# Pairing the weight-stationary steps of a Mamba-2 / attention trunk, and its decay differences on ScalarE

## The chip, the cores and the metric

The kernel runs on one core of one Trainium2 chip. The metric is the time of one execution on the device in microseconds (us); before the change the median of three runs is 2558.26 us (2557.04 to 2558.56).

## The reference

Two decoder layers over 256 tokens of width 2048, all in float32: a Mamba-2 mixer with a conv-gated feed-forward network, then block attention with another one. Nearly all the work is products of the 256 tokens with large weight matrices. The part that the change rewrites, besides the products, is the decay inside one chunk of 128 tokens:

```python
a_cum = jnp.cumsum(a, axis=2)
seg = a_cum[:, :, :, None] - a_cum[:, :, None, :]
decay_in = jnp.exp(jnp.where(causal, seg, -jnp.inf))
cb = jnp.einsum('bclgn,bcsgn->bclsg', c, b)
y_diag = jnp.einsum('bclsgr,bcsgrp->bclgrp', cb[..., None] * decay_in, x)
...
u = causal_dwconv(x @ w_up, conv_w, conv_b)
return (jax.nn.silu(gate) * val) @ w_down
```

There are 8 groups of 8 heads and two chunks of 128 tokens, so a group has 2 x 8 difference matrices of 128x128.

## The kernel before

**Products.** Weights come from HBM in tiles of 512 KB (`raw`, one per *step*; 882 steps). `split()` turns a tile into two: ScalarE casts it to `hi` (fp32r, L183), VectorE subtracts to get the rest `lo` (L184), and the next load is issued on SyncE's queue. Activations are kept the same way, as a hi half and a lo half side by side (`hT`). A product is hi·hi + lo·hi + hi·lo.

A *chunk* of steps computes 512 columns. In mode "X" the activations are the stationary operand and the weight tile streams, 12 matmuls of 512 columns a step (L206, L207, L211). In mode "W" the weights are stationary: for each of a step's eight 128x128 blocks there is one matmul of `hi` with both halves of the activations, 512 columns (L243), and one of `lo` with the hi half, 256 columns (L245). A "W" chunk has eight steps, the first four into one PSUM pair and the last four into another. `whole(i)` issues a step: in even steps the eight of `hi` and then the eight of `lo`, in odd steps the other way round, so that runs of sixteen of a kind arise. 61 chunks are of this sort: 3 for B and C and 8 for x in the Mamba layer, 42 in the two feed-forward networks, 8 for keys and queries. The first chunk (`both`) and the small one for dt (mode "H") are cut otherwise.

**Order of the work.** The program is one list of steps. In the middle of a step (after 6 of its 16 matmuls) `splits(i)` issues the split three steps ahead; there are four buffers each for `hi` and `lo`, and a split needs the buffers of the step four before it. Work of the layers is hung on steps by hand: `at(i, f)` runs f after step i. Every engine works its own list in the order of issue.

**Mamba.** Group g has an x chunk (steps `s0` to `s0+7`, mode "W") and a z chunk (`s0+8` to `s0+15`, mode "X"). Its work is hung at `s0+k`:

- `s0+3` `m_load`: DMAs on GpSimd's queue put the cumulative sums, the same for all partitions, into `mA`, one 128x1024 tile for each of two chunks of tokens (2 buffers).
- `s0+6` `m_cb`: three small matmuls (L673, L674), then `cb` on VectorE (L676) and `bc` on ScalarE (L680); `m_decay` for chunk 0: VectorE subtracts `aux` from `mA` (L685) and takes the minimum with 0 (L686). `s0+7`: the same for chunk 1, and `m_exp` for chunk 0 (ScalarE, L690); `s0+8` `m_exp` for chunk 1.
- `s0+4`, `s0+5` and `s0+8`, `s0+9`: `gather` (L550, L551) and `taps` of the convolution (ScalarE L573, then VectorE L578).
- `s0+12` silu; `s0+13`, `s0+14` the mask; `s0+15` to `s0+29` the rest of the group beside the next group's steps, among it `y_off` and `y_diag` (PE L732, L724) after the next group's third and fourth step, `z_gate` (VectorE L744, ScalarE L747) after its sixth, `z_rms` after its seventh and `z_turn` (PE L340) after the fifth and sixth steps of its z chunk.

The time steps of all groups (dt) are worked out beside the chunks of C; `dt_turn` (PE L647) comes after the third step of the second of them and needs an exponential on ScalarE (L640, L641).

Of the kernel before, what the change touches and what calls it, by code (L numbers as in the profile page):

```python
# [20 lines left out]
AF = mybir.ActivationFunctionType  # L21
OP = mybir.AluOpType
AX = mybir.AxisListType

P = 128
D = 2048
S = 256
# [31 lines left out]
def chunks():  # L59

    z, b, c, dt = 0, 2 * DI, 2 * DI + NG * DS, 2 * DI + 2 * NG * DS

    def some(mode, name, layer, c0, n, nk):
        return [(mode, name, layer, c0 + i * NC, nk, False) for i in range(n)]

    def ffn(layer):
        up = [some(m, "ffn_w_up", layer, c + j * NC, 1, KD)[0] for j in range(DFF // NC)
              for m, c in (("W" if j else "X", 0), ("W", DFF))]
        return up + some("X", "ffn_w_down", layer, 0, 4, KF)

    out = some("W", "mamba_w_in", 0, b, 2, KD)
    out[0] = out[0][:5] + (True,)
    out += some("H", "mamba_w_in", 0, dt, 1, KD) + some("W", "mamba_w_in", 0, c, 2, KD)
    for g in range(NG):
        out += some("W", "mamba_w_in", 0, DI + g * NC, 1, KD) + some("X", "mamba_w_in", 0, z + g * NC, 1, KD)
    out += some("X", "mamba_w_out", 0, 0, 4, DI // P) + ffn(0)
    out += some("X", "w_kv", None, D, 1, KD) + some("W", "w_kv", None, 0, 4, KD) + some("W", "attn_w_q", 0, 0, 4, KD)
    return out + some("X", "w_kv", None, D + NC, 3, KD) + some("X", "attn_w_o", 0, 0, 4, KD) + ffn(1)


def cut(mode, nk, both):

    if mode == "H":
        return [(0, NC // 8, k, 8) for k in range(0, nk, 8)]
    if mode == "W" and not both:
        return [(half, HC, k, 4) for half in (0, HC) for k in range(0, nk, 4)]
    return [(0, NC, k, 2) for k in range(0, nk, 2)]
# [3 lines left out]
def yoco_kernel(ctx: ExitStack, tc: tile.TileContext, x, lmg, lmb, lfg, lfb, x_t, columns, w, out):  # L91
    nc = tc.nc
# [10 lines left out]
    def acc_pair():  # L103
        return psum.tile([P, 2, NC], F32, tag="acc", name="acc", bufs=3)
# [19 lines left out]
    steps, plan = [], chunks()  # L124

    class Chunk:
# [9 lines left out]
        def __init__(self, x, head=0, tail=0):  # L136
            self.mode, _, _, _, self.nk, self.both = plan.pop(0)
            self.x, self.head, self.tail = x, head, tail
            self.cut = cut(self.mode, self.nk, self.both)
            self.n = len(self.cut)  # L140
            self.per = self.cut[0][3]
            self.nj = max(self.cut[0][1] // P, 1)
            self.first = len(steps)
            for s in range(self.n):
                steps.append((self, s))
            self.end = len(steps)
            self.last = self.end - 1

        def place(self, s):

            return self.cut[s][2], self.cut[s][0] // HC

        def ready(self, half):

            return self.end - (self.n // 2 if half == 0 and not self.both else 0)

    raw_t, hi_t, lo_t = {}, {}, {}
    spare = {}
    calm = []
# [12 lines left out]
    def split():  # L172
        i = pos["split"]
        pos["split"] += 1
        t = raw_t.pop(i)
        if i in spare:
            h, l = (bufs["h"][:, k:k + 2].rearrange("p k a t -> p k (a t)") for k in (spare[i], spare[i] + 2))
        else:
            h = wts.tile([P, 2, NC], F32R, tag="hi", name="hi")
            l = wts.tile([P, 2, NC], F32R, tag="lo", name="lo")  # L180
        for e in ((0,), (1,)) if i < 2 else ((0, 1),):
            sl = slice(e[0], e[-1] + 1)
            nc.scalar.copy(h[:, sl], t[:, sl])  # L183
            nc.vector.tensor_sub(l[:, sl], t[:, sl], h[:, sl].bitcast(F32))  # L184
        hi_t[i], lo_t[i] = h, l
        load()

    def splits(i, most=2):

        for _ in range(1 if steps[i][0] in calm else most):  # L190
            j = pos["split"]
            ahead = LA + 1 + sum(i <= k < j for k in spare)
            if j < min(i + ahead, n_steps) and (j in spare or sum(k not in spare for k in hi_t) < LA + 1):
                split()
# [27 lines left out]
    def done(i):  # L222
        hi_t.pop(i), lo_t.pop(i)

    def whole(i):
        ch, s = steps[i]
        h, l = hi_t[i], lo_t[i]
        nj = ch.nj
        h, l = (t.rearrange("p a (k n) -> p (a k) n", n=nj * P) for t in (h, l))
        k0, half = ch.place(s)  # L230
        banks = [p[:, j, :] for p in ch.part[half:] for j in range(2)]

        parts = (1, 0) if s % 2 and ch not in calm else (0, 1)
        order = [(p, kk, j) for p in parts for kk in range(ch.per) for j in range(nj)]
        for n, (p, kk, j) in enumerate(order):
            if n == len(order) * 3 // 8:
                run(mid, i)
                splits(i)
            k = k0 + kk
            begins, ends = k == 0 and p == parts[0], k == ch.nk - 1 and p == parts[1]  # L240
            js = slice(j * P, (j + 1) * P)
            if p == 0:
                nc.tensor.matmul(banks[j], h[:, kk, js], ch.x.both(k), start=begins, stop=ends, skip_group_check=True)  # L243
            else:
                nc.tensor.matmul(banks[j][:, :S], l[:, kk, js], ch.x.hi(k), start=begins, stop=ends,  # L245
                                 skip_group_check=True)

    def products(i):
        ch, s = steps[i]
        if ch.mode == "W":  # L250
            if s == 0:
                ch.part = []
            if s == 0 or (not ch.both and s == ch.n // 2):
                ch.part += [acc_pair() for _ in range(1 + ch.both)]
        elif s == 0:
            a = acc_pair()
            ch.part = [a[:, 0, :], a[:, 1, :]] if ch.mode == "X" else [a]
            if ch.tail:
                ch.part.pop()
                ch.piece = [tp_tile()[:, :HC] if ch.tail == LAST else acc_pair()[:, 0, :HC] for _ in range(2)]  # L260
        if ch.mode != "X":
            whole(i)
            return done(i)
        half(i, 0)
        if i >= ch.end - ch.tail:
            if i < ch.last:
                return splits(i)
            for q in range(2):
                for j in range(ch.end - ch.tail, ch.end):
                    half(j, 1, q)  # L270
                    if q:
                        done(j)
        elif s < ch.head - 1:
            if ch.tail:
                splits(i)
        elif s == ch.head - 1:
            for j in range(ch.first, i + 1):
                if j < i or ch.tail:
                    splits(i, 1)
                second(j)  # L280
                done(j)
            if not ch.tail:
                splits(i, 1)
        else:
            run(mid, i)
            splits(i)
            second(i)
            done(i)

    post, pre, mid, inner, outer = {}, {}, {}, {}, {}  # L290

    def run(d, i):
        for f, a in d.get(i, []):
            f(*a)

    def at(i, f, *a):
        post.setdefault(i, []).append((f, a))
# [246 lines left out]
    aux = mp.tile([P, 6, NH], F32, name="aux")  # L544
# [136 lines left out]
        G[g]["cb"], G[g]["bc"] = cb, bc  # L681

    def m_decay(g, c):
        t = G[g]["A", c]
        nc.vector.tensor_sub(t, t, aux[:, 2 + c, 8 * g:8 * g + 8].unsqueeze(2).to_broadcast([P, 8, P]))  # L685
        nc.vector.tensor_scalar(t, t, 0.0, None, op0=OP.min)  # L686

    def m_exp(g, c):
        t = G[g]["A", c]
        nc.scalar.activation(t, t, AF.Exp)  # L690

    def m_mask(g, c):
        t = G[g]["A", c]
# [81 lines left out]
    for g in range(NG):  # L775
        s0 = chX[g].first
        at(s0 + 3, m_load, g)
        at(s0 + 6, m_cb, g)
        at(s0 + 6, m_decay, g, 0)
        at(s0 + 7, m_decay, g, 1)  # L780
        at(s0 + 7, m_exp, g, 0)
        at(s0 + 8, m_exp, g, 1)
        conv4(chX[g], 4 * g, lambda g=g: x_new(g), 0).plan()
        at(s0 + 12, x_silu, g)
        at(s0 + 13, m_mask, g, 0)
        at(s0 + 14, m_mask, g, 1)
        at(s0 + 15, x_turn, g)
        at(s0 + 16, x_dt, g)
        at(s0 + 16, z_silu, g)
        at(s0 + 18, y_off, g)  # L790
        at(s0 + 18, y_diag, g, 0)
        at(s0 + 19, y_diag, g, 1)
        at(s0 + 21, z_gate, g)
        at(s0 + 22, z_rms, g)
        at(s0 + 23, z_scale, g)
        at(s0 + 28, z_turn, g, 0)
        at(s0 + 29, z_turn, g, 1)
# [213 lines left out]
    for h in range(HEADS):  # L1011
        i, j = divmod(h, 4)
# [87 lines left out]
```

## Time and profile before

| | |
|---|---|
| median of three runs | 2558.26 us |
| the profiled execution: its time / its span | 2558.33 us / 2556.4 us |
| granted TensorE clock | 0.999 |
| TensorE (PE) busy | 99% |
| VectorE (DVE) / ScalarE (ACT) busy | 65% / 51% |
| share of the DMA engines, mean rate | 61%, 196 GB/s |
| the chain that ended last | PE 98%, DVE 1% |

Busy shares are of the span. Matmuls overlap in the pipeline, so a PE that is busy all the time can still have lost time between matmuls; start-to-start times tell it. In rows of the timeline the columns are start, duration of the merged instructions, engine, line, operation, out<-in, shapes, count, and in brackets how long the engine sat idle before and what ended that.

### The profile page before, as it was taken

What the parts mean: (1) busy time and instruction counts of PE and PEld (TensorE: products, weight loads), DVE (VectorE), ACT (ScalarE), POOL (GpSimd) and SP (SyncE); (2) the same over time, 40 slices, a digit from 0 to 9 for tenths busy, and PEclk for the clock granted to TensorE, in tenths of its full rate; (3) what the DMA queues carried; (4) which work ended last, traced back from release to release, by engine and by line L of the source; (5) the groups of instructions that cost most, each with busy time, mean ns of one, the idle gap of its engine ahead of it and who ended that gap; (6) DMA issues with size and microseconds to landing.
All of it is one profiled execution on the core that took longest, in us unless ns stands there. A gap on an engine that the chain in (4) does not pass through costs nothing.

```text
span 2556.4 us, 35404 instructions
## 1 busy us (share of the span) xinstructions
PE 2543.6 (99%) x13744; PEld 2199.0 (86%) x13744; DVE 1666.5 (65%) x2138; ACT 1300.0 (51%) x1634; POOL 72.3 (3%) x87
## 2 busy tenths in 40 slices
PE   9999999999999999999999999999999999999998
PEld 8888888888888888888888888888888888888887
DVE  6877788854676666666444745655777676765545
ACT  6656556633465555555333444543555555554333
POOL 0000000000200000000000200000200000000001
PEclk9999999999999999999999999999999999999999
DMA  7555555557566565666676655456665666566675
GB/s 260 197 186 188 189 179 186 192 186 234 185 228 190 187 190 184 194 192 190 199 229 199 222 190 173 157 173 223 222 197 187 192 186 192 185 195 200 198 224 163
DMA packets 141495, 500.98 MB, mean 196 GB/s; under 512 B 15616, under 2 KB 16128, under 8 KB 141328
## 3 DMA queue, kind: packets, MB, share of 16 engines
q1 hardware_dynamic: 136976, 483.46, 58.8%
q0 software_dynamic: 4064, 14.75, 1.8%
q8 instruction: 107, 1.75, 0.3%
q14 instruction: 60, 0.49, 0.1%
q10 hardware_dynamic: 288, 0.52, 0.1%
HBM read 490.22 MB, written 8.45 MB: 195 GB/s over the span
## 4 chain that ended last, share of the span: by engine, by line
PE 98%; DVE 1%; issue 0%; ACT 0%; DMA 0%; SPq 0%; DVEq 0%
PE acc L243 36%; PE acc L245 19%; PE acc L211 13%; PE acc L206 13%; PE acc L207 13%; PE tp L724 1%; PE tp L211 0%; PE tp L207 0%; PE tp L206 0%; DVE lo L184 0%; PE tp L340 0%; PE tp L708 0%; PE tp L965 0%; PE tp L732 0%; DVE r L417 0%
## 5 line engine op out<-in xcount | busy, mean ns | idle before, releaser
L184 DVE TENSOR_TENSOR lo<-raw,hi 128x1024 fp32r<-128x1024 f32 (+1 forms) x871 | 1063.2, 1226 | 732.2 <-ACT hi L183 728.3
L183 ACT CAST hi<-raw 128x1024 fp32r<-128x1024 f32 (+1 forms) x871 | 912.6, 1049 | 915.6 <-PE acc L211 377.4
L243 PE MATMUL acc<-hT,hi 128*128 128x512 f32 x3984 | 961.4, 392 | 0.4 <-ACT hi L183 0.4
L243 PEld LDWEIGHTS acc<-hT,hi 128*128 128x128 f32 x3984 | 731.0, 188 | 141.7 <-ACT hi L183 1.0
L245 PEld LDWEIGHTS acc<-hT,lo 128*128 128x128 f32 x3984 | 512.5, 191 | 20.0
L245 PE MATMUL acc<-hT,lo 128*128 128x256 f32 x3984 | 522.5, 283 | 0.0
L207 PE MATMUL acc<-lo,gT 128*128 128x512 f32 (+1 forms) x678 | 254.5, 378 | 0.0
L206 PE MATMUL acc<-hi,gT 128*128 128x512 f32 (+1 forms) x678 | 254.1, 377 | 0.0
L211 PE MATMUL acc<-hi,gT 128*128 128x512 f32 (+1 forms) x678 | 200.8, 377 | 0.0
L206 PE MATMUL acc<-hi,hT 128*128 128x512 f32 x448 | 179.9, 402 | 0.0
L207 PE MATMUL acc<-lo,hT 128*128 128x512 f32 x448 | 175.2, 391 | 0.0
L207 PEld LDWEIGHTS acc<-lo,gT 128*128 128x128 f32 x678 | 127.7, 188 | 23.4
L206 PEld LDWEIGHTS acc<-hi,gT 128*128 128x128 f32 x678 | 127.5, 188 | 23.0
L211 PEld LDWEIGHTS acc<-hi,gT 128*128 128x128 f32 x678 | 124.9, 188 | 23.7
L211 PE MATMUL acc<-hi,hT 128*128 128x512 f32 x448 | 139.4, 392 | 0.6 <-DVE hT L353 0.6
L211 PEld LDWEIGHTS acc<-hi,hT 128*128 128x128 f32 x448 | 83.4, 188 | 20.5 <-DVE hT L353 3.0
L206 PEld LDWEIGHTS acc<-hi,hT 128*128 128x128 f32 x448 | 84.2, 188 | 17.2 <-ACT hT L352 1.3
L206 PE MATMUL acc<-hi,yT 128*128 128x512 f32 (+1 forms) x270 | 98.9, 371 | 0.0
L207 PEld LDWEIGHTS acc<-lo,hT 128*128 128x128 f32 x448 | 84.3, 188 | 16.9 <-DVE lo L184 0.9
L207 PE MATMUL acc<-lo,yT 128*128 128x512 f32 (+1 forms) x270 | 98.6, 369 | 0.0
L211 PE MATMUL acc<-hi,yT 128*128 128x512 f32 (+1 forms) x270 | 77.7, 369 | 0.0
L578 DVE SCALAR_TENSOR_TENSOR g<-u,cols,g 128x254 f32<-128x254 f32 (+1 forms) x176 | 73.5, 478 | 5.3 <-ACT g L573 5.3
(200 smaller groups left out, 1875.6 us busy)
## 6 DMA issues: line engine op xcount, KB each, us to landing
raw<-in_w SPq DMA_DIRECT2D x881, 512.0 KB, 4.1
mA<-acum_d POOLq DMA_DIRECT2D x16, 512.0 KB, 5.2
hres<-r POOLq DMA_DIRECT2D x12, 512.0 KB, 6.3
r<-hres SPq DMA_DIRECT2D x12, 512.0 KB, 5.1
r<-in_x SPq DMA_DIRECT2D x4, 512.0 KB, 5.2
gb<-in_ln_mix_g SPq DMA_DIRECT2D x8, 256.0 KB, 6.0
gb<-in_ln_mix_b SPq DMA_DIRECT2D x8, 256.0 KB, 6.4
gb<-in_ln_ffn_g SPq DMA_DIRECT2D x8, 256.0 KB, 5.5
```

Of the source, the lines that this page charges most:

```text
L183: nc.scalar.copy(h[:, sl], t[:, sl])
L184: nc.vector.tensor_sub(l[:, sl], t[:, sl], h[:, sl].bitcast(F32))
L206: nc.tensor.matmul(a, th, h[:, kk, sl], start=k == 0, stop=False)
L207: nc.tensor.matmul(a, th, l[:, kk, sl], start=False, stop=False)
L211: nc.tensor.matmul(a, ch.x.lo(k)[:, ts], h[:, kk, sl], start=False, stop=k == ch.nk - 1)
L243: nc.tensor.matmul(banks[j], h[:, kk, js], ch.x.both(k), start=begins, stop=ends, skip_group_check=True)
L245: nc.tensor.matmul(banks[j][:, :S], l[:, kk, js], ch.x.hi(k), start=begins, stop=ends, skip_group_check=True)
L578: nc.vector.scalar_tensor_tensor(d, u[:, i % 2, :S - k], c1(self.at_w, w[n - 1 - k] + self.ia + i), d, op0=OP.mult, op1=OP.add)
L724: nc.tensor.matmul(ps[:, h * 64:(h + 1) * 64], G[g]["A", c][:, h, :], G[g]["xdt"][:, c, h * 64:(h + 1) * 64], start=True, stop=True)
```

## The change

Two edits. **Pairs:** in the 61 chunks of mode "W" the steps are issued two by two. The even step of a pair issues the first kind of product for both steps (sixteen matmuls), the odd step the second kind for both. The first and third pair of a chunk begin with `hi`, the second and fourth with `lo`. The even step's tiles are given up in the middle of the odd step, and the odd step's split is issued there. **Decays:** `m_decay` becomes eight ScalarE activations, one for each head (128x128, Relu of `-mA + aux`, with a bias of one value per partition); `m_exp` takes the sign back with a scale of -1 and moves one step later, to `s0+8` and `s0+9`.

```diff
+            self.paired = self.mode == "W" and not self.both
...
+        def kinds(self, s):
+            return (1, 0) if (s // 2 if self.paired else s) % 2 and self not in calm else (0, 1)
...
-    def whole(i):
-        parts = (1, 0) if s % 2 and ch not in calm else (0, 1)
-        order = [(p, kk, j) for p in parts for kk in range(ch.per) for j in range(nj)]
-        for n, (p, kk, j) in enumerate(order):
-            if n == len(order) * 3 // 8:
-                run(mid, i)
-                splits(i)
...
+    def whole(i):
+        ch, s = steps[i]
+        a, b = ch.kinds(s)
+        if not ch.paired:
+            order = [(s, a), (s, b)]
+        elif s % 2 == 0:
+            order = [(s, a), (s + 1, a)]
+        else:
+            order = [(s - 1, b), (s, b)]
+        late = ch.paired and s % 2
+        n = len(order) * ch.per * ch.nj
+        c = 0
+        for t, p in order:
+            for _ in some(ch, t, p):
+                if c == (n // 2 if late else n * 3 // 8):
+                    if late:
+                        done(i - 1)
+                    run(mid, i)
+                    splits(i)
+                c += 1
+        if not ch.paired or late:
+            done(i)
...
     def m_decay(g, c):
         t = G[g]["A", c]
-        nc.vector.tensor_sub(t, t, aux[:, 2 + c, 8 * g:8 * g + 8].unsqueeze(2).to_broadcast([P, 8, P]))
-        nc.vector.tensor_scalar(t, t, 0.0, None, op0=OP.min)
+        for h in range(8):
+            nc.scalar.activation(t[:, h, :], t[:, h, :], AF.Relu, scale=-1.0, bias=aux[:, 2 + c, 8 * g + h:8 * g + h + 1])
...
-        nc.scalar.activation(t, t, AF.Exp)
+        nc.scalar.activation(t, t, AF.Exp, scale=-1.0)
...
-        at(s0 + 7, m_exp, g, 0)
-        at(s0 + 8, m_exp, g, 1)
+        at(s0 + 8, m_exp, g, 0)
+        at(s0 + 9, m_exp, g, 1)
```

`some(ch, s, p)` yields before each matmul of step s and kind p; the matmuls themselves are those of before.

More of the change, by code (lines that the diff above doesn't have):

```diff
@@ L223, in done, with some @@
         hi_t.pop(i), lo_t.pop(i)
+    def some(ch, s, p):
+        i = ch.first + s
+        nj = ch.nj
+        w = ((hi_t, lo_t)[p][i]).rearrange("p a (k n) -> p (a k) n", n=nj * P)
+        k0, half = ch.place(s)
+        banks = [p[:, j, :] for p in ch.part[half:] for j in range(2)]
+        first = ch.kinds(s)[0] == p
+        for kk in range(ch.per):
+            k = k0 + kk
+            begins, ends = first and k == 0, not first and k == ch.nk - 1
+            for j in range(nj):
+                yield
+                js = slice(j * P, (j + 1) * P)
+                if p == 0:
+                    nc.tensor.matmul(banks[j], w[:, kk, js], ch.x.both(k), start=begins, stop=ends,
+                                     skip_group_check=True)
+                else:
+                    nc.tensor.matmul(banks[j][:, :S], w[:, kk, js], ch.x.hi(k), start=begins, stop=ends,
+                                     skip_group_check=True)
@@ L225, in whole @@
     def whole(i):
         ch, s = steps[i]
[L227 to L231, printed above, removed]
-        parts = (1, 0) if s % 2 and ch not in calm else (0, 1)
-        order = [(p, kk, j) for p in parts for kk in range(ch.per) for j in range(nj)]
-        for n, (p, kk, j) in enumerate(order):
-            if n == len(order) * 3 // 8:
-                run(mid, i)
-                splits(i)
[L239 to L246, printed above, removed]
+        a, b = ch.kinds(s)
@@ new lines, in whole @@
+        if not ch.paired:
+            order = [(s, a), (s, b)]
+        elif s % 2 == 0:
+            order = [(s, a), (s + 1, a)]
+        else:
+            order = [(s - 1, b), (s, b)]
[10 more added lines that the diff above has]
+                c += 1
@@ L261, in products @@
         if ch.mode != "X":
-            whole(i)
-            return done(i)
+            return whole(i)
         half(i, 0)
```

## The prediction

> **What bounds the kernel now.** I read the page first, then the list of waits, the chain that ended last, and the timeline of a few stretches.
>
> ```profile
> span 2556.4 us, 35404 instructions
> PE 2543.6 (99%) x13744; PEld 2199.0 (86%) x13744; DVE 1666.5 (65%) x2138; ACT 1300.0 (51%) x1634; POOL 72.3 (3%) x87
> ```
> ```profile
> PEld acc L211 <- DVE hT L353: 3.0, 6, 0.6
> ```
>
> The first fence is the page, the second the longest of all entries in the list of waits in which TensorE waits: 3.0 us in all. So the span is the PE's own instructions. Two things can move the time: the start-to-start time of matmuls, and waits of the PE that are not there now. The profiled execution took 2558.33 us, 1.9 more than its span and 0.07 more than the median of three, so a change of the span can be added to either. About 0.2% (5.1 us) is what a measurement here can tell from no change.
>
> **Pairs, on the PE itself.** No matmul is added or removed; only the changes between kinds are halved. Timeline of single runs of a kind, and the chain:
>
> ```profile
> 1500.36 1.75 PE L243 MATMUL acc<-hT,hi 128*128 128x512 f32 x7
> ```
> ```profile
> 1503.23 1.24 PE L245 MATMUL acc<-hT,lo 128*128 128x256 f32 x9
> ```
> ```profile
> 734.87 3.65 PE acc L243 x16
> 746.00 3.65 PE acc L243 x16
> ```
>
> Inside a run one matmul of 512 columns follows another after (1.75-0.39)/6 = 0.227 us, one of 256 after (1.24-0.28)/8 = 0.120 (0.39 and 0.28 are the durations of the last of each run, which count once). Four steps are 32 of each: 32 x 0.2267 + 32 x 0.120 = 11.09 us. The chain shows 11.13 from one run to the next but one: 0.04 us for four changes of kind. Pairing takes away four of a chunk's eight changes, so 0.04 us a chunk, **61 x 0.04 = 2.5 us saved**. The Trainium skill (TensorE: Matmul & The Clock Gate, "Back-to-back issue gap") makes the gap a function of the columns alone, N/2.4 + 2.5 ns; by it the order of kinds is free, and the sum below would be 2.5 us more, 2583. The 0.04 us of the rows speak against that, by little.
>
> **Pairs, on the buffers.** With Δ = 8 x (0.227-0.120) = 0.85 us, what stands on the PE's list after an even step comes Δ later in a pair that begins with hi and Δ earlier in one that begins with lo. In a lo-first pair both steps' lo products are needed eight hi products earlier, 8 x 0.227 = 1.8 us; in a hi-first pair both steps' lo buffers come free eight hi products later, 1.8 us too (the even step's after 16 of hi and 8 of lo instead of 8 and 8). The cover for this in the feed-forward stages, timeline there:
>
> ```profile
> 771.23 1.22 DVE L184 TENSOR_TENSOR lo<-raw,hi 128x1024 fp32r<-128x1024 f32 x1 [2.40 <-ACT hi L183]
> 777.32 2.08 PE L245 MATMUL acc<-hT,lo 128*128 128x256 f32 x16
> ```
>
> This lo tile is ready at 772.45 and used by the second eight of that run, at 778.28: 5.8 us of lead, of an odd step in a lo-first pair, the kind that loses most. Less 1.8 for the earlier use and at most 1.8 for VectorE standing behind a later buffer, 2 us stay. I cost the pairing at nothing there. If that cover is gone, it is the third rival. The loads move with their splits by no more than 1.8 us; they have four raw buffers on SyncE's queue.
>
> **Decays.** Rows by shape, and ScalarE's timeline in the dt stage, which has the nearest activations:
>
> ```profile
> L685 DVE TENSOR_TENSOR mA<-mA,aux 128x1024 f32<-128x1024 f32 x16 | 19.4, 1215 | 0.0
> L686 DVE TENSOR_SCALAR mA<-mA 128x1024 f32<-128x1024 f32 x16 | 11.1, 694 | 0.5
> ```
> ```profile
> 87.06 0.40 ACT L640 ACTIVATE tb<-tb 64x128 f32<-64x128 f32 x1 [6.33 <-DVE tb L638]
> 87.38 0.31 ACT L641 ACTIVATE tb<-tb 64x128 f32<-64x128 f32 x1
> 87.59 0.56 ACT L550 COPY u<-acc 128x512 f32<-128x512 f32 x1
> ```
>
> VectorE loses 1.2 + 0.7 = 1.9 us for each of 16 calls. ScalarE gets eight activations of 128 columns. L640 has a bias per partition, as they have, and holds the engine 0.32 us; L641 has none and holds it 0.21; without any overlap it would be 0.40. I take 0.32, since L640 is the same form: **2.56 us a call**, bounds 1.7 and 3.2. The Trainium skill (ScalarE: Activation LUTs, "Rules for kernel authors") advises VectorE, not ScalarE, for relu and min; that rule speaks against this edit, and the rows agree with it, 1.9 us there against 2.56 here. What the move costs is told by the stretch after a group's `m_cb`, in three views of one steady group, PE, VectorE, ScalarE:
>
> ```profile
> 265.51 2.07 PE L243 MATMUL acc<-hT,hi 128*128 128x512 f32 x8
> ...
> 291.68 0.40 PE L207 MATMUL acc<-lo,hT 128*128 128x512 f32 x1
> ```
> ```profile
> 268.70 1.22 DVE L184 TENSOR_TENSOR lo<-raw,hi 128x1024 fp32r<-128x1024 f32 x1 [0.54 <-ACT hi L183]
> 269.84 1.22 DVE L744 TENSOR_TENSOR xs<-xs,sz 128x1024 f32<-128x1024 f32 x1
> 272.96 2.55 DVE L578 SCALAR_TENSOR_TENSOR xc<-u,cols,xc 128x255 f32<-128x255 f32 x6 [1.90 <-ACT xc L573]
> ...
> 276.63 0.41 DVE L676 TENSOR_TENSOR cb<-tp,tri 128x256 f32<-128x256 f32 x1
> ...
> 286.38 2.45 DVE L578 SCALAR_TENSOR_TENSOR xc<-u,cols,xc 128x255 f32<-128x255 f32 x6
> 288.75 3.49 DVE L184 TENSOR_TENSOR lo<-raw,hi 128x1024 fp32r<-128x1024 f32 x3
> ```
> ```profile
> 272.34 1.08 ACT L573 ACTIVATE xc<-u,cols 128x256 f32<-128x256 f32 x2
> ...
> 277.08 0.27 ACT L680 COPY bc<-tp 128x128 f32<-128x128 f32 x1 [2.73 <-DVE cb L676]
> 277.24 1.05 ACT L183 CAST hi<-raw 128x1024 fp32r<-128x1024 f32 x1
> 278.31 1.28 ACT L690 ACT_TABLE_LOAD   x1
> 279.61 1.07 ACT L690 ACTIVATE mA<-mA 128x1024 f32<-128x1024 f32 x1
> 280.58 1.03 ACT L183 CAST hi<-raw 128x1024 fp32r<-128x1024 f32 x1
> 282.73 1.06 ACT L690 ACTIVATE mA<-mA 128x1024 f32<-128x1024 f32 x1 [1.11 <-DVE mA L686]
> 283.69 0.57 ACT L550 COPY u<-acc 128x512 f32<-128x512 f32 x1
> 284.16 1.05 ACT L183 CAST hi<-raw 128x1024 fp32r<-128x1024 f32 x1
> 285.11 1.09 ACT L573 ACTIVATE xc<-u,cols 128x256 f32<-128x256 f32 x2
> ```
>
> The x chunk's third pair begins at 265.51, the same as after the change, for as many matmuls and inserted products lie ahead of it. Step 1: the lo split of step `s0+8` (268.70) needs the lo buffer of `s0+4`, the first of that pair. After the change this is read until 265.51 + 16 x 0.227 + 8 x 0.12 = 270.1, and with the last matmul's 0.28 less its 0.12 the split starts at 270.36: VectorE waits, **1.66 us later**. Behind it on VectorE stand the gate (269.84), for whose result ScalarE's squares and taps wait (272.34), the taps for those (272.96), then `cb` (276.63), and for `cb` waits `bc` on ScalarE (2.73 us idle). Each is followed by the next, so `bc` moves from 277.08 to 278.74. The matrices `mA` are there: the second is loaded from 266.0, when L724 is over, with the 5.2 us to landing of this row of the page:
>
> ```profile
> mA<-acum_d POOLq DMA_DIRECT2D x16, 512.0 KB, 5.2
> ```
>
> Step 2, ScalarE's list in its new order with start-to-start times of the rows: `bc` 278.74 (+0.16), eight decays (+2.56), cast (+0.95), eight decays (+2.56), cast (+1.07), table load (+1.30), exp (+0.96), copy (+0.47), cast (+0.95), exp (+0.97), so the convolution's taps start at **290.69 instead of 285.11**. VectorE's taps follow 0.62 later (as 272.34 to 272.96), and 2.37 after their start (286.38 to 288.75) the lo split of `s0+13` starts: 293.68, done 294.90. VectorE's own relief is worth nothing here, as it waits for ScalarE. The PE needs this tile at 291.68, or 291.64 with the 0.04 saved: **3.3 us of waiting**. The lo splits of `s0+10` to `s0+12` are late on the way too, by less, and these waits are part of the 3.3, since nothing in ScalarE's list up to here waits for the PE. ScalarE is busy 51% of the span and VectorE 65%, so I let both catch up before the next group. Groups 1 to 7: **7 x 3.3 = 23.1 us**.
>
> Group 0 has no gate of an earlier group; VectorE and PE there:
>
> ```profile
> 122.79 0.42 DVE L676 TENSOR_TENSOR cb<-tp,tri 128x256 f32<-128x256 f32 x1 [1.15 <-PE tp L674]
> ...
> 134.13 2.35 DVE L184 TENSOR_TENSOR lo<-raw,hi 128x1024 fp32r<-128x1024 f32 x2
> ```
> ```profile
> 139.15 0.39 PE L207 MATMUL acc<-lo,hT 128*128 128x512 f32 x1
> ```
>
> `cb` moves by 1.66 less the 1.15 of waiting, 0.5; from `cb` to that lo split it was 11.34 and becomes 0.45 + 14.94 = 15.39, so 4.05 more; the tile was ready at 135.35, 3.76 before its use less 0.04: **0.8 us**. One more place, in the dt stage:
>
> ```profile
> 87.85 0.59 PE L647 MATMUL tp<-ident,tb 64*128 64x64 f32 x6
> ```
>
> This transpose stands after an even step of a lo-first pair, so it comes 0.85 earlier, while its operand is written by L641 until 87.69, now 0.16 ahead of it: **0.9 us**, bounds 0 and 2. Sum: -2.5 + 23.1 + 0.8 + 0.9 = **+22.3 us, 2580.6, say 2581 us** (+0.9%).
>
> **The rivals.** *Not slower:* ScalarE's list is not what is last. `s0+13` had 1.7 us of lead (288.75 + 1.22 against 291.68). If the decays pass at 0.21 us, 1.76 a group is gone, and if the lo buffer does not hold the gate, another 1.66: 3.3 - 3.4 is nothing, and with the dt wait of 0.9 the saving leaves 2556.7. It decides from about 0.9 us a group down, where the sum is within 5.1 us. For it: all of it is one chain of eleven small steps; against it: each half alone leaves 1.5 us a group or more. *Relu wants a table load of its own:* no Relu is in the trace; a load holds ScalarE 1.30 us (278.31 to 279.61). One more ahead of the decays: 7 x 1.3 + 1.3 more, 2591. Against it: the casts and copies between L690 and the next silu cause none. By the Trainium skill (same page, "Table sets") relu is in every set, so there would be none; its price for a switch ("What ACT_TABLE_LOAD costs"), 2.66 us, is twice what the row shows. *The weight buffers bind everywhere:* if the 2 us of cover in the other 53 chunks fail, each of two lo-first pairs waiting 0.1 to 0.2 us costs 11 to 21 more, some 2597. Against it: the 5.8 us above.
>
> **How the numbers follow.** Forecast 0.72, table load 0.08, buffers 0.08, not slower 0.12. The forecast's own bounds: at 0.21 us an activation 1.5 x 7 + 0 + 0.9 - 2.5, 2567; at 0.40 4.6 x 7 + 2.1 + 0.9 - 2.5, 2591; without the gate's shift 1.6 x 7, 2569. The range 2565 to 2595 takes these in, the table load too, and leaves out "not slower" and the worst of the buffers. Slower 0.86 (2 in 100 of the forecast's low end fall within 0.2%), same 0.11, faster 0.03, which needs more than the 2.5 us that I can find.
>
> **What would show it.** Right: waits of TensorE for `lo` L184 in the z chunks, some 20 us in all and some 3 in each from group 1 on, the last before the fifth or sixth step's second matmul; eight Relu rows of about 0.4 us each, 0.32 apart; `bc` 1.7 us later against its chunk; runs of 32 of a kind in the feed-forward stages without waits, and a chunk of 22.2 us there. Wrong: no wait of the PE for lo in the z chunks, table loads other than 8 and 8 at L690 and L701, or waits spread over the feed-forward chunks.

## The result and the profile after

The changed kernel takes **2581.08 us** (median of four runs, 2580.43 to 2581.70), the kernel before 2557.97 (2557.04 to 2558.56, four runs). The ratio is 1.0091, with a 95% interval of 1.0073 to 1.0108: slower by 23 us. The profiled execution took 2581.7 us, 1.9 more than its span.

The page of the changed kernel, its first lines and the shares of the chain that ended last:

```profile
span 2579.8 us, 35509 instructions
PE 2551.9 (99%) x13744; PEld 2199.7 (85%) x13744; DVE 1636.1 (63%) x2106; ACT 1331.2 (52%) x1762; POOL 72.2 (3%) x87
PE 90%; ACT 4%; DVE 4%; issue 2%; DMA 0%; SPq 0%; DVEq 0%; ACTq 0%
```

Busy times hardly move: ScalarE gains 31 us, VectorE loses 30, and PE is at 99% in both. The chain tells more. Before it was PE with 98%; now 8% of it lie on ScalarE and VectorE. The list of waits says where they hand over (sum in us, times, the longest; PEld is the weight load ahead of a matmul):

```profile
PEld acc L213 <- DVE lo L190: 25.3, 32, 1.1
PE acc L213 <- DVE lo L190: 13.6, 28, 0.8
PEld acc L249 <- DVE lo L190: 2.1, 2, 1.1
PE acc L249 <- DVE lo L190: 1.7, 2, 0.9
```

Before, no wait of TensorE in this list was over 3.0 us. L213 is the second matmul of a step of the z chunks (L207 before): four waits in each of the groups 1 to 7. L249 is the `lo` product of the weight-stationary chunks, which waits just twice, both times in the dt stage.

Subtracting the start of each chunk before from its start after gives the course of the loss. Up to the second chunk of C the shift is -0.23 us; across that chunk, beside which dt ends, +3.65; group 0 +0.30; each of groups 1 to 7 +3.11 to +3.15, together 21.9; from the first feed-forward chunk to the end -2.2, 0.04 for nearly every paired chunk. The sum, 23.4, is the difference of the spans. The x chunks of groups 1 to 7 are paired too and gain nothing: each takes 27.50 us, where it was 27.49.

**One group.** This is the group quoted in the prediction. Its x chunk starts with these rows of PE, before and after:

```profile
249.91 2.10 PE L243 MATMUL acc<-hT,hi 128*128 128x512 f32 x8
```
```profile
259.86 3.92 PE L246 MATMUL acc<-hT,hi 128*128 128x512 f32 x16
```

ScalarE's timeline of the changed kernel in it:

```profile
288.79 0.27 ACT L707 COPY bc<-tp 128x128 f32<-128x128 f32 x1 [2.73 <-DVE cb L703]
288.96 2.46 ACT L714 ACTIVATE mA<-mA,aux 128x128 f32<-128x128 f32 x8
291.31 1.04 ACT L189 CAST hi<-raw 128x1024 fp32r<-128x1024 f32 x1
292.25 2.46 ACT L714 ACTIVATE mA<-mA,aux 128x128 f32<-128x128 f32 x8
295.66 1.28 ACT L718 ACT_TABLE_LOAD   x1
300.29 1.08 ACT L600 ACTIVATE xc<-u,cols 128x256 f32<-128x256 f32 x2
```

`bc` stands 28.93 us after the start of its x chunk; before it was 277.08 - 249.91 = 27.17. From `bc` to the taps it takes 11.50 us; before 285.11 - 277.08 = 8.03. VectorE and PE of the same group:

```profile
280.41 1.23 DVE L190 TENSOR_TENSOR lo<-raw,hi 128x1024 fp32r<-128x1024 f32 x1 [2.28 <-issue]
303.38 3.49 DVE L190 TENSOR_TENSOR lo<-raw,hi 128x1024 fp32r<-128x1024 f32 x3
```
```profile
293.66 0.50 PE L213 MATMUL acc<-lo,hT 128*128 128x512 f32 x1 [0.47 <-DVE lo L190]
296.95 0.50 PE L213 MATMUL acc<-lo,hT 128*128 128x512 f32 x1 [0.27 <-DVE lo L190]
300.74 0.51 PE L213 MATMUL acc<-lo,hT 128*128 128x512 f32 x1 [0.72 <-DVE lo L190]
304.65 0.50 PE L213 MATMUL acc<-lo,hT 128*128 128x512 f32 x1 [0.44 <-DVE lo L190]
```

The first VectorE row is the held subtraction of `s0+8`: 20.55 us into the x chunk, 18.79 before. The row names no releaser (`issue`); that it waits for its buffer is shown below, by the run in which it has one of its own. The second ends its first tile, that of `s0+13`, at 304.60, and the last of the four PE rows uses it at 304.65. The four waits show 1.9 us of idle PE, and the steps behind them come 0.77, 0.60, 1.05 and 0.73 later, 3.15 in all. The rest is lost overlap: without a wait a matmul of 0.39 us is followed by the next after 0.23, so 0.16 of it is hidden, and the matmul behind a wait takes 0.50, its weight load beginning only when it does (293.66 for the first). For the first wait 0.47 + 0.16 + 0.11 is 0.74 us.

**Feed-forward.** PE's timeline there, four steps in each pair of rows:

```profile
780.68 7.44 PE L246 MATMUL acc<-hT,hi 128*128 128x512 f32 x32
...
802.91 7.44 PE L246 MATMUL acc<-hT,hi 128*128 128x512 f32 x32
```

Runs of 32 of a kind, no waits, 22.23 us for eight steps, where it was twice 11.13.

### The profile page after: what moved, and what is told of

The parts are those of the page before. It is cut to its first block, busy times and chain, and to the rows that moved or that the text cites. A ratio compares the mean times of both kernels' runs of the same rounds, so it can differ in the third digit from the quotient of the medians.

```text
span 2579.8 us, 35509 instructions
## 1 busy us (share of the span) xinstructions
PE 2551.9 (99%) x13744; PEld 2199.7 (85%) x13744; DVE 1636.1 (63%) x2106; ACT 1331.2 (52%) x1762; POOL 72.2 (3%) x87
## 3 DMA queue, kind: packets, MB, share of 16 engines
q8 instruction: 107, 1.75, 0.3%
## 4 chain that ended last, share of the span: by engine, by line
PE 90%; ACT 4%; DVE 4%; issue 2%; DMA 0%; SPq 0%; DVEq 0%; ACTq 0%
PE acc L246 33%; PE acc L249 17%; PE acc L213 12%; PE acc L217 12%; PE acc L212 12%; DVE lo L190 1%; ACT mA L714 1%; ACT hi L189 1%; DVE xc L605 1%; PE tp L752 1%; ACT mA L718 1%; PE tp L217 0%; PE tp L213 0%; PE tp L212 0%; ACT L718 0%
## 5 line engine op out<-in xcount | busy, mean ns | idle before, releaser
L246 PE MATMUL acc<-hT,hi 128*128 128x512 f32 x3984 | 938.0, 391 | 0.2 <-ACT hi L189 0.2
L246 PEld LDWEIGHTS acc<-hT,hi 128*128 128x128 f32 x3984 | 739.2, 188 | 149.0 <-ACT hi L189 1.1
L249 PEld LDWEIGHTS acc<-hT,lo 128*128 128x128 f32 x3984 | 496.6, 192 | 12.5 <-DVE lo L190 2.1
L249 PE MATMUL acc<-hT,lo 128*128 128x256 f32 x3984 | 502.2, 283 | 1.7 <-DVE lo L190 1.7
L213 PE MATMUL acc<-lo,gT 128*128 128x512 f32 (+1 forms) x678 | 254.5, 378 | 0.0
L213 PE MATMUL acc<-lo,hT 128*128 128x512 f32 x448 | 178.5, 398 | 13.6 <-DVE lo L190 13.6
L213 PEld LDWEIGHTS acc<-lo,gT 128*128 128x128 f32 x678 | 127.7, 188 | 23.3
L213 PEld LDWEIGHTS acc<-lo,hT 128*128 128x128 f32 x448 | 84.2, 188 | 40.6 <-DVE lo L190 25.3
L213 PE MATMUL acc<-lo,yT 128*128 128x512 f32 (+1 forms) x270 | 98.6, 369 | 0.0
L578 DVE TENSOR_TENSOR u<-u,acc 128x512 f32<-128x512 f32 x108 | 73.5, 681 | 13.8 <-ACT u L577 13.8
```

Of the source, the lines that this page charges most:

```text
L213: nc.tensor.matmul(a, th, l[:, kk, sl], start=False, stop=False)
L246: nc.tensor.matmul(banks[j], w[:, kk, js], ch.x.both(k), start=begins, stop=ends, skip_group_check=True)
L249: nc.tensor.matmul(banks[j][:, :S], w[:, kk, js], ch.x.hi(k), start=begins, stop=ends, skip_group_check=True)
L578: nc.vector.tensor_add(dst, dst, p[:, :, :S])
```

## The experiments

Each experiment is the changed kernel with the edit shown, unless it says otherwise. Times are medians; the kernel before beside them has a median of 2558.0 over all the runs.

**One half of the change at a time.** First pairs without the decays: `m_decay` and `m_exp` as before, on VectorE and at their old steps.

```diff
-        for h in range(8):
-            nc.scalar.activation(t[:, h, :], t[:, h, :], AF.Relu, scale=-1.0, bias=...)
+        nc.vector.tensor_sub(t, t, aux[:, 2 + c, 8 * g:8 * g + 8].unsqueeze(2).to_broadcast([P, 8, P]))
+        nc.vector.tensor_scalar(t, t, 0.0, None, op0=OP.min)
```

> Pairs as in the change, decays and exp as before on VectorE. Theory (lead used up by a chain): in each group the gate and so bc still come 1.7 us later, but the lo split of s0+13 had 1.7 us of lead, so a group waits 0 to 0.3 us; what is left is the dt stage, 3.7, and the saving of 2.5: some +2 us, 2560. Rival (each edit costs its own delay): the 1.7 us are lost in each of seven groups, +13 us, 2571. Decisive: TensorE's waits for lo in the z chunks.

Measured 2559.95 us (2559.47 to 2562.37), ratio 1.0009 (0.9999 to 1.0018). That is the theory's 2560, not the rival's 2571. Groups 1 to 7 lose 0.20 to 0.24 us each, the second chunk of C, beside which dt ends, 2.83; 0.04 comes back in nearly every paired chunk outside Mamba.

Then the decays without pairs:

```diff
-            self.paired = self.mode == "W" and not self.both
+            self.paired = False
```

> Steps not paired, decays on ScalarE and exp a step later as in the change. Theory: two calls of 2.35 us lengthen ScalarE's list after bc, less the 1.1 that it waited for VectorE's decays and what VectorE's taps waited for the lo split; the lo split of s0+13 comes about 2.9 us later against 1.7 of lead, 1.2 to 1.3 us a group, 0 in group 0, +9 us, 2567. Rival (each edit costs its own delay): 2.9 a group, +20, 2578. By the theory the losses of e1 and e2 do not add up to the change's 23 us.

Measured 2567.39 (2567.24 to 2567.70), ratio 1.0037 (1.0023 to 1.0051). That is the theory's 2567, not the rival's 2578. Groups 1 to 7 lose 1.35 each, that chunk of C 0.00. The longest entry of TensorE in its list:

```profile
PEld acc L213 <- DVE lo L190: 11.8, 18, 0.8
```

So the halves alone cost 1.9 and 9.3 us, 11 together, and the change 23. Each half can spend the same lead of the `lo` tile of `s0+13` (the time from when it is ready to its use), which the prediction put at 1.7 us (288.75 + 1.22 against 291.68); together they can spend it only once. In a group 0.21 + 1.35 = 1.56, and 3.13 together: 1.6 more.

**The hold.** Step 1 of the prediction says that the gate, `cb` and `bc` come late because the subtraction of `s0+8` waits for its buffer. The gate ahead of it:

```diff
-        at(s0 + 21, z_gate, g)
+        at(s0 + 20, z_gate, g)
```

> The change, with z_gate hung one step earlier (after s0+20 instead of s0+21), so that on VectorE it stands ahead of the lo split of the next s0+8, which waits for its buffer. Theory: bc comes up to 3 us earlier and the z chunks lose 0 to 0.4 us a group instead of 3.1; the dt stage's 3.7 and the saving stay, 2559 to 2562. Rival (the decays on ScalarE are the loss, whatever stands before them): 2578 to 2581.

Measured 2566.34 (2566.02 to 2568.29), ratio 1.0034 (1.0022 to 1.0045): between the two, a miss for both. Groups 1 to 7 lose 1.03 to 1.07 each. ScalarE's timeline, x chunk from 254.63:

```profile
273.53 0.63 ACT L775 ACTIVATE sz<-xs 128x512 f32<-128x512 f32 x1 [3.74 <-DVE xs L772]
...
274.77 0.56 ACT L577 COPY u<-acc 128x512 f32<-128x512 f32 x1
275.24 1.05 ACT L189 CAST hi<-raw 128x1024 fp32r<-128x1024 f32 x1
...
281.48 0.27 ACT L707 COPY bc<-tp 128x128 f32<-128x128 f32 x1 [3.26 <-DVE cb L703]
```

The gate's squares now stand ahead of the gather's copy and of the cast of `s0+8`, so the subtraction behind them is late for another reason: it waits for this cast. `bc` comes 26.85 us into its chunk, 2.1 earlier than in the change, and the loss falls by 2.1. Getting the gate out from behind the hold is worth that much, but the decays still cost what is left, which the expectation had taken for nearly nothing. This run moved two things at once, so a cleaner run followed, in which only the hold goes: the subtraction of `s0+8` gets a buffer of its own.

```diff
-            l = wts.tile([P, 2, NC], F32R, tag="lo", name="lo")
+            own = any(i == c.first for c in chZ)
+            l = mp.tile([P, 2, NC], F32R, tag="lo5", name="lo5") if own else wts.tile([P, 2, NC], F32R, tag="lo", name="lo")
```

> The change as it is, but the lo half of step s0+8 of each group has a buffer of its own, so its subtraction no longer waits for the third pair of the x chunk; the order of ScalarE's list stays. My theory, in two steps: the hold goes, `bc` comes about 1.7 us earlier against its chunk than in the change (where it was 28.9 us after the start of the x chunk), and of the 3.13 us a group those 1.4 to 1.7 that the decays alone cost are left: 2570 us, between 2568 and 2572. Rival, ScalarE's list alone makes the whole loss and the hold is covered: groups stay at 3.1 and the time at 2581. Second rival, from the run with the gate moved, where a group kept 1.0: if that is what is left without the hold, 2566.

Measured 2568.83 (2568.30 to 2569.24), ratio 1.0043 (1.0029 to 1.0056), as the theory had it. VectorE's and ScalarE's timelines, x chunk from 255.02 (line numbers are one higher in this kernel):

```profile
273.84 1.23 DVE L191 TENSOR_TENSOR lo<-raw,hi 128x1024 fp32r<-128x1024 f32 x1 [0.55 <-ACT hi L190]
```
```profile
282.22 0.27 ACT L708 COPY bc<-tp 128x128 f32<-128x128 f32 x1 [2.73 <-DVE cb L704]
```

The subtraction starts 18.82 us into the chunk, as before the change; what it waits for is its cast, no longer its buffer. `bc` is at 27.20, and groups 1 to 7 lose 1.37 to 1.41. Taking the hold away gains 1.7 us a group; the rest is the decays.

**ScalarE's time.** Step 2 says that this rest is the time of the activations on ScalarE's list. Four activations in place of eight:

```diff
-        for h in range(8):
-            nc.scalar.activation(t[:, h, :], t[:, h, :], ...)
+        for h in range(0, 8, 2):
+            nc.scalar.activation(t[:, h:h + 2, :], t[:, h:h + 2, :], ...)
```

> The change, with four activations of 256 columns in place of eight of 128 for each decay call; each pair of heads then uses the bias of its first head, so the values of every second head are not the reference's. ScalarE's rows give 0.294 us from one 128-column activation to the next and about 0.96 for 1024 columns, so about 0.39 for 256: a call takes 1.56 us instead of 2.35, two calls 1.6 less a group. My theory, ScalarE's time between `bc` and the taps is passed on to TensorE one for one: seven groups of 1.5 instead of 3.1, 2570 us. Rival, the loss comes from where the decays stand or from what the pairs do to the buffers, not from how long they take: 2580 to 2581.

Measured 2569.71 (2569.41 to 2572.95), ratio 1.0049 (1.0035 to 1.0063). ScalarE's timeline, x chunk from 258.40:

```profile
287.33 0.27 ACT L707 COPY bc<-tp 128x128 f32<-128x128 f32 x1 [2.72 <-DVE cb L703]
287.50 1.71 ACT L714 ACTIVATE mA<-mA,aux 128x256 f32<-128x256 f32 x4
289.11 1.03 ACT L189 CAST hi<-raw 128x1024 fp32r<-128x1024 f32 x1
```

`bc` is at 28.93, exactly as in the change, a call holds ScalarE 1.61 us instead of 2.35, and groups 1 to 7 lose 1.62 to 1.66 instead of 3.13: 1.48 us less on ScalarE's list, 1.5 less a group. The list is passed on one for one.

These kernels in one table, each from its profile, `bc` in the same group. Its rows with pairs alone (x chunk from 252.30) and with the decays alone (from 252.39):

```profile
281.23 0.27 ACT L707 COPY bc<-tp 128x128 f32<-128x128 f32 x1 [2.72 <-DVE cb L703]
```
```profile
279.56 0.27 ACT L707 COPY bc<-tp 128x128 f32<-128x128 f32 x1 [2.73 <-DVE cb L703]
```

| kernel | `bc` after the start of its x chunk, us | a decay call on ScalarE, us | loss of a group, us |
|---|---|---|---|
| before | 27.17 | none | 0 |
| pairs alone | 28.93 | none | 0.2 |
| decays alone | 27.17 | 2.35 | 1.35 |
| gate earlier | 26.85 | 2.35 | 1.05 |
| own buffer | 27.20 | 2.35 | 1.4 |
| four activations | 28.93 | 1.61 | 1.6 |
| the change | 28.93 | 2.35 | 3.13 |

In the four rows with 2.35 us a call, each 0.1 us of `bc` is about 0.1 us of loss.

**The dt stage.** The chunks of B and C without pairs:

```diff
-            self.paired = self.mode == "W" and not self.both
+            self.paired = self.mode == "W" and not self.both and len(steps) >= 34
```

> The change, but the three chunks of B and C that were paired are not. Theory: the 3.65 us that the second chunk of C lost go, and 0.12 us of saving with them; the groups stay at 3.1 each: 2577.5. Rival (the dt stage's loss is the transpose that stands after an even step, and the buffers have no part): the cast held for its hi buffer is not the cause, and 0.9 go, 2580.5.

Measured 2577.99 (2577.57 to 2579.60), ratio 1.0079 (1.0064 to 1.0094). The second chunk of C loses 0.02, groups 1 to 7 3.1 as in the change, and L249 no longer waits for `lo`. So this loss comes from the pairs in the chunks of B and C, and it is more than the rival's 0.9.

**The gain.** Is it the number of changes of kind that costs PE the 0.04 us? The kernel before, with twice as many:

```diff
-        parts = (1, 0) if s % 2 and ch not in calm else (0, 1)
+        parts = (0, 1)
```

> The kernel before, but every step of a weight-stationary chunk does its 512-column products first and its 256-column ones second, so a chunk has sixteen changes of kind instead of eight. By the 0.04 us that four fewer changes saved in each chunk of the run with pairs, eight more cost 0.08 us a chunk, 62 chunks 5 us: 2563. Rival, the saving in the pairs came from something else than the number of changes (the gap depends on the columns alone): 2558.

Measured 2562.29 (2561.98 to 2562.89, 11 runs), ratio 1.0017 (1.0008 to 1.0026). PE's timeline in the feed-forward stage, eight steps from the first row to the second:

```profile
770.22 2.00 PE L243 MATMUL acc<-hT,hi 128*128 128x512 f32 x8
...
792.57 2.00 PE L243 MATMUL acc<-hT,hi 128*128 128x512 f32 x8
```

A chunk takes 22.35 us; by the starts of the chunks it was 22.27 with eight changes and is 22.23 with four: 0.01 us a change, in both directions. The theory had 2563, the rival 2558.

**What is left when the losses go.** Pairs everywhere but in B and C, decays as before, the gate one step earlier:

```diff
+            self.paired = self.mode == "W" and not self.both and len(steps) >= 34
...
+        nc.vector.tensor_sub(t, t, aux[:, 2 + c, 8 * g:8 * g + 8].unsqueeze(2).to_broadcast([P, 8, P]))
+        nc.vector.tensor_scalar(t, t, 0.0, None, op0=OP.min)
...
+        at(s0 + 20, z_gate, g)
```

> Only the part that saves: pairs in every weight-stationary chunk except those of B and C, the decays and exps as before on VectorE, and the gate one step earlier, ahead of the subtraction that pairs hold up. 58 chunks of 0.04 us less and no loss in the dt stage or in the groups: -2.3 us, 2555.8. Rival, the earlier gate pushes something else in the groups: the 0.2 us a group of the run with pairs alone stays or grows, 2557 to 2559.

Measured 2556.08 (2555.32 to 2556.76, 11 runs), ratio 0.9992 (0.9983 to 1.0001). Its list has one entry for `lo`, three waits in all, the same as the kernel before:

```profile
PEld acc L213 <- DVE lo L190: 0.9, 3, 0.3
```

Groups 1 to 7 lose 0.01 each, and nearly every paired chunk from the first feed-forward one on gains 0.04, 2.2 us to the end. The forecast of 2555.8 fits, but by time alone the interval does not tell this kernel from the one before.

## Why the prediction was right, and where its terms were off

It had 2581 us, 22.3 more than before. Both steps of the mechanism hold, and one small term was wrong by more than its bound.

- **Groups 1 to 7: 3.3 us each, measured 3.13.** Step 1 put `bc` 1.66 later against its chunk; it is 1.76 later. (Its terms add up to 270.26 for the start of the subtraction, not to the 270.36 that it states, so they give 1.56.) Step 2 put the taps at 290.69, which is 40.78 after the start of the x chunk; they start 300.29 - 259.86 = 40.43 after it. The difference is the activation, sixteen times 0.026 us less, against the 0.10 more of `bc`: 0.32 us was taken from L640, and the eight follow one another in 2.35 us, 0.294 each. The lookup that would have given it: the Trainium skill (ScalarE: Activation LUTs, "What ACT_TABLE_LOAD costs") has 280 ns plus 0.833 ns a column with a bias per partition, less 93 ns of overlap back to back; worked out, that is an estimate of 294 ns for 128 columns and 400 for 256. The trace agrees: 0.294, and 1.61 / 4 = 0.40 with 256 columns.
- **Group 0: 0.8, measured 0.3.** Sixteen activations that take 0.026 us less each are 0.4 of the 0.5.
- **Pairs, on the PE: -2.5; measured 0.04 a chunk, 2.2 in the chunks outside Mamba.** Twice the changes cost 0.08 us a chunk, so the order of kinds is not free here, as the rows had it. The formula of the Trainium skill weighed there (TensorE: Matmul & The Clock Gate, "Back-to-back issue gap") is given on that page for a matmul in isolation. The x chunks of groups 1 to 7 gained nothing; why is not shown.
- **Pairs, on the buffers: nothing outside Mamba.** Right: no wait for `lo` in the feed-forward or attention chunks. The rival in which the buffers bind everywhere is out.
- **The dt stage: 0.9 with bounds 0 and 2, measured 2.83 in the runs of pairs alone and own buffer, 3.65 in the profiled run of the change. This step failed.** The prediction moved the transpose by 0.85 us and left dt's own work where it was. ScalarE before and after, VectorE before and after, PE before and after:

```profile
64.75 1.05 ACT L183 CAST hi<-raw 128x1024 fp32r<-128x1024 f32 x1 [0.76 <-PE acc L243]
65.81 1.28 ACT L600 ACT_TABLE_LOAD   x1
```
```profile
66.47 1.05 ACT L189 CAST hi<-raw 128x1024 fp32r<-128x1024 f32 x1 [4.62 <-PE acc L246]
67.55 1.28 ACT L627 ACT_TABLE_LOAD   x1
```
```profile
82.70 1.21 DVE L184 TENSOR_TENSOR lo<-raw,hi 128x1024 fp32r<-128x1024 f32 x1
...
84.83 1.21 DVE L184 TENSOR_TENSOR lo<-raw,hi 128x1024 fp32r<-128x1024 f32 x1
```
```profile
84.44 1.21 DVE L190 TENSOR_TENSOR lo<-raw,hi 128x1024 fp32r<-128x1024 f32 x1
...
86.56 1.21 DVE L190 TENSOR_TENSOR lo<-raw,hi 128x1024 fp32r<-128x1024 f32 x1
87.70 0.34 DVE L661 TENSOR_SCALAR ta<-tb,an 64x256 f32<-64x256 f32 x1
```
```profile
86.81 1.11 PE L245 MATMUL acc<-hT,lo 128*128 128x256 f32 x8
...
88.37 1.21 PE L245 MATMUL acc<-hT,lo 128*128 128x256 f32 x8
```
```profile
85.70 1.22 PE L249 MATMUL acc<-hT,lo 128*128 128x256 f32 x8 [0.80 <-DVE lo L190]
87.83 1.79 PE L249 MATMUL acc<-hT,lo 128*128 128x256 f32 x8 [0.91 <-DVE lo L190]
89.55 0.90 PE L674 MATMUL tp<-ident,tb 64*128 64x64 f32 x6
```

In the first two fences a cast starts 1.7 us later, since the `hi` buffer that it waits for is read later in a pair, and behind it in the list stands dt's first exponential with its table load. In VectorE's list dt's instructions stand between the subtractions, and both subtractions come 1.73 to 1.74 us later. On the PE two `lo` products, needed 1.8 us earlier in a lo-first pair, wait for them. The 5.8 us of cover were read in the feed-forward stage alone: here the same two tiles were ready only 2.9 and 2.3 us ahead of their use (82.70 + 1.21 against 86.81, 84.83 + 1.21 against 88.37), less than the 3.5 that 1.8 and 1.7 make. So it is the mechanism of step 1, a hold with work queued behind it, which the prediction applied to the z chunks alone. That the pairs in B and C cause this loss is shown by the run without them; the way through the held cast is read from the timelines, and no run takes the hold alone away.

- **The rivals.** Not slower: it needed 0.9 us a group or less; the smallest with the decays as activations of 128 columns is 1.03. A table load for Relu: the row of all table loads behind the decays still counts 8, and none stands at L714 (line, engine, operation, count, duration min/median/max in ns):

```profile
L718 ACT ACT_TABLE_LOAD  x8: 1283/1283/1283, 133.7 to 512.3; - x8
```

That the total met the forecast within a microsecond owes something to luck: the groups were 0.17 us too dear seven times and group 0 by 0.5, the dt stage 1.9 too cheap.

## What to carry to other kernels

When a reordering makes a buffer free later, look up which instruction waits for that buffer, on which engine, and what stands behind it in that engine's list: the hold is paid by them, and it is paid at every place where long work is queued behind, not just at the one that is examined. Two changes that spend the same lead cost more together (3.13 us a group here) than the sum of what each costs alone (0.21 and 1.35); cost them against one lead, once. Work moved to a half idle engine is paid in full if it lands on the stretch of that engine's list that feeds the critical one.

## What the hardware showed that was not expected

After the two short waits in the dt stage the granted clock fell to half in some executions. In all ten profiles the clock changes only at whole multiples of 3.413 us from its first change; in the change that first one is at 6.27 us, and the fall to half comes 24 such stretches later, at 88.19. The stretch with the waits and the one after it (busy time of PE, PEld, DVE, ACT, POOL, then the granted clock, DMA share and GB/s), the change and then pairs alone:

```profile
84.78:88.19 3.41, 1.70 (x13) 1.38 (x12) 3.38 (x7) 0.00 (x0) 0.00 (x0) 1.00 0.73 274
88.19:91.60 3.41, 3.41 (x17) 2.88 (x16) 2.27 (x5) 2.81 (x6) 0.75 (x1) 0.50 0.55 185
```
```profile
83.61:87.02 3.41, 1.90 (x14) 1.49 (x13) 3.38 (x6) 0.00 (x0) 0.00 (x0) 1.00 0.76 229
87.02:90.43 3.41, 3.20 (x20) 2.70 (x21) 2.27 (x7) 2.23 (x5) 0.75 (x1) 1.00 0.77 249
```

The same two waits, 0.80 or 0.81 and 0.91 us, stand in five profiles. In the change and with four activations both fall, all but 0.05 us, into one stretch, PE is busy for 1.70 and 1.75 of its 3.41 us, and the next stretch runs at half. With pairs alone, with the own buffer and with the earlier gate the edge of a stretch cuts through the second wait or between the two, PE is busy for at least 1.90, 1.92 and 2.51, and the clock stays at 1.00. The first change of the clock is at 4.65 to 6.27 us of the span in these five, so where the edges fall differs from run to run. In these five profiles the line thus lies between 1.75 and 1.90 us of 3.41; no run was made to test it.

In the change the clock was at half for one stretch, 3.41 us, which fits the 0.8 us by which 3.65 exceeds 2.83; its other three runs have spans 0.8 to 1.2 us shorter. With four activations it was two stretches, and the second chunk of C lost 5.2. The Trainium skill (TensorE: Matmul & The Clock Gate, "What's actually happening") has the clock halved after an idle window of about 3.4 us, in a window that runs on its own. The trace agrees with the length and with a window that runs on its own, but PE was idle for only 1.71 and 1.66 us of the two windows that were followed by it. The four waits in each z chunk, 0.27 to 0.72 us of idle, were not followed by it.

The other: a wait of PE costs more than the idle time in its row. The 15.3 us in PE's entries for `lo` went with some 25 us of shift, and the weight loader's entries, 27.4, are the nearer measure.
